# Matmuls on part of TensorE's array are widened to the whole array, with zeros where rows were missing

## The chip, the cores and the metric

The kernel runs on one core of a Trainium2 chip. The metric is the device time of one execution in microseconds (us): 2548.41, the median of three runs (2547.5 to 2549.49).

## The reference

Two transformer-like layers act on 512 tokens of width 1024, all in 32-bit floats. The first has a pooling branch, a gated delta rule with 8 heads of 128 and a product-key expert layer. The second has a state-space scan with 16 heads of 64 and a stick-breaking attention with 16 heads of 64. Three pieces matter here:

```python
# delta rule and scan: decay between two positions of a chunk, per head
diff = gc[..., :, None] - gc[..., None, :]
decay = jnp.where(tril, jnp.exp(jnp.where(tril, diff, 0.0)), 0.0)
# stick breaking, per head
logits = jnp.einsum('bqhd,bkhd->bhqk', q, k) * scale
log_fail = jnp.where(mask, jax.nn.log_sigmoid(-logits), 0.0)
between = lax.cumsum(log_fail, axis=3, reverse=True) - log_fail
w = jnp.where(mask, jnp.exp(jax.nn.log_sigmoid(logits) + between), 0.0)
out = jnp.einsum('bhqk,bkhd->bqhd', w, v)
```

## The kernel before

Activations are kept with features on partitions. A projection takes a slab of weights (128 x 1024), brought by SyncE's DMA into `raw`, rounded by ScalarE into a high part `wh`, whose rest `wl` is made by GpSimd or VectorE; then 24 matmuls of 512 columns add high x high, high x low and low x high into one PSUM tile (`pf` by features, `pt` by tokens). The order of all instructions is fixed when the program is written: generators are advanced between matmuls by a model of time (`K.mm` adds the matmul's columns, `Engine` the VectorE and ScalarE work), and inside each engine the order is then kept. `K.mm` (line 175) counts columns and type alone.

TensorE's array has 128 rows (the contraction, operand partitions) and 128 columns (outputs, PSUM partitions). The profile prints both for each matmul: 64*128 is 64 rows and 128 columns.

The change touches three helpers and their callers.

- `widen`, `decay_rows` and `decay` (lines 1506 to 1530): for H heads the per-token rates are copied to columns 0 to H-1 and 32 to 32+H-1 of a zeroed tile `gw`. `decay_rows` multiplies them with a triangle into `pgr`, rows 0 to 32+H-1, and ScalarE copies these into `gr`, in a rounded high part and, on rows 32 and up, a low part made by VectorE. `decay` then makes one head's table `pd`: a mask by a bf16 matmul, plus a matmul whose stationary operand is one column of `pick`, repeated 128 times, over 40 (H = 8, delta heads) or 48 (H = 16, scan) partitions; `pick` has a one in rows h and 32+h of column h and zeros elsewhere. ScalarE exponentiates `pd` into `DT`. Eight heads do this near 59 to 76 us and 266 to 277 us, sixteen from 1952 to 2019 us, each between projection matmuls.
- `qk_slab` in `block2_` (line 1624): a slab gives queries or keys of two heads, 64 features each. Head 0 has partitions 0 to 63, head 1 has 64 to 127. Tiles `qa` and `qb` hold a head's high part; for queries the other 64 partitions get the low part by a DMA, for keys they get the high part again. The keys' low parts lie in one tile `ql` for both heads.
- `stick` (line 1951): one generator for each of the two heads ("lanes"), over 8 feature slabs; a unit below is one lane in one slab, 16 in all. Its steps: masks (`msb`, 4 bf16 matmuls) and logits, `psb`, for four key blocks of 512, 384, 256 and 128 queries, each with a full matmul (high and repeated keys against high and low queries) and one over the head's 64 partitions (low keys); VectorE and ScalarE make softplus, in high and low parts `sbh`, `sbl`; the cumulative sum on TensorE with a triangle `trilr` and a block of minus ones `nonesr`, into the same `psb`; the exponential `sbw` on ScalarE; the weighted values, four f32 matmuls (two passes each in the trace) with 64 columns of the values `v2t`; and a product with the gate, `og`, on VectorE. Steps of the two lanes stand among the 24 matmuls of the next slabs' projections.

```python
# L1971: logits of one key block, full and half
self.mm(ps[:, c:c + n], k[:, ks], q[:, kb * 128:512], start=False, stop=False, skip_group_check=True)
self.mm(ps[:, c:c + n], kl[ds, ks], q[ds, kb * 128:512], start=False, stop=False, skip_group_check=True)
```

Of the kernel before, what the change touches and what calls it, by code (L numbers as in the profile page):

```python
# [9 lines left out]
F32 = mybir.dt.float32  # L10
F32R = mybir.dt.float32r
# [13 lines left out]
NT = 4  # L25
H1 = 8
# [62 lines left out]
class K:  # L89
# [568 lines left out]
    def decay_rates(self, pba, narrow):  # L658
        yield from narrow
        nc, sm = self.nc, self.sm  # L660
        sh = [128, NT, H1]
        beta = sm.tile(sh, F32, name="beta")
        nc.scalar.activation(beta, pba[:, :, 0:8], AF.Exp, scale=-1.0)
        nc.vector.tensor_scalar(beta, beta, 1.0, None, op0=OP.add)
        nc.vector.reciprocal(beta, beta)
        al = sm.tile(sh, F32, name="al")
        nc.vector.tensor_tensor(al, pba[:, :, 8:16],
                                self.row[:, None, R_DTB:R_DTB + 8].to_broadcast(sh), OP.add)
        g = sm.tile(sh, F32, name="g")
        self.softplus(sm, g, al, "sp1")  # L670
        ea = sm.tile([128, H1], F32, name="ea")
        nc.scalar.activation(ea, self.row[:, R_AL:R_AL + 8], AF.Exp)
        nc.vector.scalar_tensor_tensor(out=g, in0=g, scalar=-1.0, in1=ea[:, None, :].to_broadcast(sh),
                                       op0=OP.mult, op1=OP.mult)
        gw = self.wk.tile([128, 512], F32, name="gw", tag="cy", bufs=5)
        gw = gw[:, :NT * (32 + H1)].rearrange("p (n h) -> p n h", n=NT)
        self.widen(gw, g, H1)
        yield from self.dve(0.3)
        gr = sm.tile([128, 512], F32R, name="gr")
        self.decay_rows(gr, gw, H1, 4)  # L680
        pg = self.pmm.tile([128, 2, NT * H1], F32, name="pg", tag="sc", bufs=4)
        self.mm(pg[:, 0, :], self.triu, g, start=True, stop=True)
        self.mm(pg[:, 1, :], self.ones, g, start=True, stop=True)
        ng = sm.tile(sh, F32, name="ng")
        nc.scalar.activation(ng, pg[:, 0, :], AF.Copy, scale=-1.0)
        eg = sm.tile(sh, F32, name="eg")
        nc.scalar.activation(eg, pg[:, 0, :], AF.Exp)
        egl = sm.tile(sh, F32, name="egl")
        nc.scalar.activation(egl, pg[:, 1, :], AF.Exp)
        gd = sm.tile(sh, F32, name="gd")  # L690
        nc.vector.tensor_tensor(gd, pg[:, 1, :], ng, OP.add)
        edl = sm.tile(sh, F32, name="edl")
        nc.scalar.activation(edl, gd, AF.Exp)
        neg = sm.tile(sh, F32, name="neg")
        nc.vector.tensor_scalar(neg, eg, -1.0, None, op0=OP.mult)
        self.dn.update(beta=beta, gr=gr, ng=ng, eg=eg, neg=neg, egl=egl, edl=edl)
        self.dump("d_beta", beta); self.dump("d_g", g)
# [814 lines left out]

    def decay_rows(self, gr, gw, nh, bufs):

        nc = self.nc
        ps = self.pmm.tile([128, 512], F32, name=self.nm("pgr"), tag="sc", bufs=bufs)
        for n in range(NT):
            self.mm(ps[0:32 + nh, n * 128:n * 128 + 128], gw[:, n, :], self.triu, start=True, stop=True)
        nc.scalar.copy(gr[0:32 + nh], ps[0:32 + nh])
        nc.vector.tensor_tensor(gr[32:32 + nh], ps[32:32 + nh], gr[32:32 + nh].bitcast(F32), OP.subtract)  # L1520

    def decay(self, pd, gr, nh, col, nb, out):

        nc = self.nc
        self.mm(pd, self.identb, self.mnegb[:, None, :].to_broadcast([128, NT, 128]),
                start=True, stop=False, skip_group_check=True)
        self.mm(pd, self.pick[0:32 + nh, col:col + 1].to_broadcast([32 + nh, 128]),
                gr[0:32 + nh].rearrange("p (n i) -> p n i", n=NT), start=False, stop=True, skip_group_check=True)
        for n in range(NT):
            nc.scalar.activation(out[:, n, :], pd[:, n, :], AF.Exp, bias=nb[:, n, col:col + 1])  # L1530

# [4 lines left out]
    def block2_(self):  # L1536
        nc, a, tc, sm, big = self.nc, self.a, self.tc, self.sm, self.big
# [3 lines left out]
        with ExitStack() as ctx:  # L1541
            wk = self.wk = ctx.enter_context(tc.tile_pool(name="swk", bufs=1))
# [13 lines left out]
            zt, yt, vt, og = TK("zt", "A"), TK("yt", "B"), TK("v2t", "H"), B8("og", "D")  # L1556
# [29 lines left out]
            for i in range(4):  # L1586
                self.proj_tok("w_z2_t", i, xn,
                              lambda t, ps, i=i: self.silu2(zt[:, t:t + 2, i * 256:i * 256 + 256], ps),
                              tag=("mm" if i else "sd", 2))
            for i in range(4):  # L1590
                self.proj_tok("w_v2_t", i, xn,
                              lambda t, ps, i=i: nc.scalar.copy(vt[:, t:t + 2, i * 256:i * 256 + 256], ps))
# [16 lines left out]
        with ExitStack() as ctx:  # L1609
            wk = self.wk = ctx.enter_context(tc.tile_pool(name="bwk", bufs=1))  # L1610
# [8 lines left out]
            nc.scalar.preload_act_table_set("natural_log_exp_and_others")  # L1619
            self.qk = {}  # L1620
            lanes = [self.stick(s_, vt, og, oh, ol) for s_ in range(2)]
            go = lambda s_: next(lanes[s_], None)

            def qk_slab(f, which, mid):
                def put(j, ps):

                    scale = (0.125, 1.0)[which]
                    T = lambda n, b=1: wk.tile([128, 512], F32R, name=self.nm(n), tag=f"{n}{which}", bufs=b)
                    hl, lo = (T("qa"), T("qb", 2 - which)), T("ql")
                    half = (slice(0, 64), slice(64, 128))  # L1630
                    for s_ in range(2):
                        nc.scalar.activation(hl[s_][half[s_]], ps[half[s_]], AF.Copy, scale=scale)
                        if which:
                            nc.scalar.dma_start(out=hl[s_][half[1 - s_]].bitcast(F32), in_=hl[s_][half[s_]].bitcast(F32))

                    def rest():
                        for s_ in range(2):
                            nc.vector.scalar_tensor_tensor(out=lo[half[s_]], in0=ps[half[s_]], scalar=scale,
                                                           in1=hl[s_][half[s_]].bitcast(F32), op0=OP.mult, op1=OP.subtract)
                        if not which:  # L1640
                            for s_ in range(2):
                                nc.sync.dma_start(out=hl[s_][half[1 - s_]].bitcast(F32), in_=lo[half[s_]].bitcast(F32))
                    self.rest = rest
                    self.qk[f, which] = hl, lo
                self.proj_feat("w_in2_t", [12 + 2 * f + which], xn, put, mid=mid)
# [53 lines left out]
        with ExitStack() as ctx:  # L1699
            wk = self.wk = ctx.enter_context(tc.tile_pool(name="cwk", bufs=1))  # L1700
            self.pmm = ctx.enter_context(tc.tile_pool(name="cps", bufs=1, space=PSUM))
            out = TK("out2", "F")
# [92 lines left out]
    def scan_rates(self, xn):  # L1795

        nc, a, sm, wk = self.nc, self.a, self.sm, self.wk
# [3 lines left out]
        T = lambda n, dt=F32: sm.tile(sh, dt, name=n)  # L1801
        r = self.sr = {n: T(n) for n in ("dt", "ncs", "ecs", "egl", "dtd")}

        def rates():
# [9 lines left out]
            nc.vector.scalar_tensor_tensor(out=ad, in0=r["dt"], scalar=-1.0, in1=ea[:, None, :].to_broadcast(sh),  # L1814
                                           op0=OP.mult, op1=OP.mult)
            gw = wk.tile([128, 512], F32, name="gw2", tag="cy", bufs=5)
            gw = gw[:, :NT * 48].rearrange("p (n h) -> p n h", n=NT)
            self.widen(gw, ad, 16)
            yield from self.dve(0.8)
            r["gr"] = wk.tile([128, 512], F32R, name="gr2", tag="gr2")  # L1820
# [130 lines left out]
    def stick(self, s_, vt, og, oh, ol):  # L1951

        nc, wk = self.nc, self.wk
        ds = slice(64 * s_, 64 * s_ + 64)
# [3 lines left out]
        W = lambda n, dt=F32: wk.tile([128, 1280], dt, name=self.nm(n), tag=n, bufs=1)  # L1958
        for f in range(8):
            q, (k, kl) = self.qk[f, 0][0][s_], self.qk[f, 1]  # L1960
            k = k[s_]
            ps = self.pmm.tile([128, 3, 512], F32, name=self.nm("psb"), tag=f"sb{s_}", bufs=1)
            ps = ps.rearrange("p b c -> p (b c)")
            for kb in range(NT):
                c, n = seg[kb]
                self.mm(ps[:, c:c + 128], self.identb, self.msb, start=(kb != 3), stop=False, skip_group_check=True)
            for kb in range(NT):
                c, n = seg[kb]
                ks = slice(kb * 128, kb * 128 + 128)
                self.mm(ps[:, c:c + n], k[:, ks], q[:, kb * 128:512], start=False, stop=False, skip_group_check=True)  # L1970
                self.mm(ps[:, c:c + n], kl[ds, ks], q[ds, kb * 128:512], start=False, stop=False, skip_group_check=True)  # L1971
            e = W("sbe")
            for p in parts:
                nc.vector.tensor_scalar(e[:, p], ps[:, p], 60.0, None, op0=OP.min)
# [3 lines left out]
            hi, lo = W("sbh", F32R), W("sbl", F32R)  # L1978
# [7 lines left out]
            for t_ in (hi, lo):  # L1986
                for kb in range(NT):
                    c, n = seg[kb]
                    for kk in range(kb, NT):
                        cc, nn = seg[kk]  # L1990
                        self.mm(ps[:, c + n - nn:c + n], self.trilr if kk == kb else self.nonesr, t_[:, cc:cc + nn],
                                start=False, stop=(kk == NT - 1 and t_ is lo), skip_group_check=True)
            e = W("sbw")
            for p in parts:
                nc.scalar.activation(e[:, p], ps[:, p], AF.Exp)
            yield
            h = 2 * f + s_
            for kb in range(NT):
                c, n = seg[kb]
                self.mm(ps[ds, kb * 128:512], vt[:, kb, h * 64:h * 64 + 64], e[:, c:c + n],  # L2000
                        start=(kb == 0), stop=(kb == NT - 1), skip_group_check=True)
            nc.vector.tensor_tensor(og[ds, f, :], og[ds, f, :], ps[ds, 0:512], OP.mult)
            if s_:
# [119 lines left out]
```

## Time and profile before

| what | value |
|---|---|
| runs, median | 2548.41 us |
| profiled execution, its time | 2550.09 us |
| its span on the core | 2548.3 us |
| TensorE matmuls (PE) busy | 2459.3 us, 97%, 13497 instructions |
| weight loads (PEld) | 2108.3 us, 83% |
| VectorE (DVE) | 1709.0 us, 67% |
| ScalarE (ACT) | 994.0 us, 39% |
| GpSimd (POOL) | 656.2 us, 26% |
| chain of waits that ended last | PE 86%, DVE 11%, issue 2% |

A matmul's row shows its start and a modelled length; matmuls are pipelined, so the distance from one start to the next is the time that one takes, not the length. In square brackets stands how long the engine was idle before an instruction and who released it; "issue" is idle time for which the profile shows no wait.

### The profile page before, as it was taken

Reading aid. Unit: us, or ns where it says so; the run is one execution under the profiler, and the core shown is the slowest. Engines: PE = TensorE matmul, PEld = TensorE weight load, DVE = VectorE, ACT = ScalarE, POOL = GpSimd, SP = SyncE. Lnnn points to the kernel's source line nnn. Section 1 sums busy time; section 2 is a strip of 40 time slices with the busy share of each in tenths; the row PEclk is TensorE's granted clock in tenths of the full one; section 3 lists DMA queues with packets and bytes.
Section 4 is the critical chain, followed back from the end, with each engine's and each line's share of the span. In section 5 each row is a group of like instructions: output and inputs, shape, how many; then the busy total and the mean of one; then the engine's idle time right before and its main releaser. Section 6 shows DMA issues by size and latency. Waiting matters only on the chain.

```text
span 2548.3 us, 34826 instructions
## 1 busy us (share of the span) xinstructions
PE 2459.3 (97%) x13497; PEld 2108.3 (83%) x13497; DVE 1709.0 (67%) x3123; ACT 994.0 (39%) x1453; POOL 656.2 (26%) x401
## 2 busy tenths in 40 slices
PE   6999999989989999999999999999799999999997
PEld 5888788888989999999888888888678988776787
DVE  6776776558998988987577777777754430455433
ACT  4532522332245546455333333333432342444432
POOL 0000000014652222322232323322335234311142
PEclk9999999999999999999999999999899999999999
DMA  3231231324778989889999999998222123222122
GB/s 116 73 93 59 77 110 50 125 101 131 245 269 295 339 286 346 317 315 360 347 326 345 334 343 340 338 323 276 78 67 67 59 91 99 78 60 63 50 91 92
DMA packets 184982, 482.41 MB, mean 189 GB/s; under 512 B 26992, under 2 KB 77296, under 8 KB 184816
## 3 DMA queue, kind: packets, MB, share of 16 engines
q1 hardware_dynamic: 143856, 342.80, 39.5%
q0 software_dynamic: 36864, 134.23, 14.6%
q10 hardware_dynamic: 4096, 3.15, 0.6%
q8 instruction: 106, 1.74, 0.3%
q14 instruction: 60, 0.49, 0.1%
HBM read 422.45 MB, written 53.48 MB: 187 GB/s over the span
## 4 chain that ended last, share of the span: by engine, by line
PE 86%; DVE 11%; issue 2%; ACT 1%; DMA 1%; POOL 0%; SPq 0%; ACTq 0%; DVEq 0%; POOLq 0%
PE pf L175 27%; PE y L175 20%; PE pa L175 18%; PE pt L175 7%; PE psb L175 5%; DVE hn L74 3%; PE pg L175 2%; DVE wl L74 1%; PE tp L180 1%; PE pd L175 1%; PE pyd L175 1%; PE pz L175 1%; DVE oh L74 1%; DVE rt L74 0%; DVE h_out L74 0%
## 5 line engine op out<-in xcount | busy, mean ns | idle before, releaser
L74 ACT CAST wh<-raw 128x1024 fp32r<-128x1024 f32 x310 | 326.4, 1053 | 681.1 <-PE pf L175 303.3
L273 POOL TENSOR_TENSOR wl<-raw,wh 128x1024 fp32r<-128x1024 f32 x113 | 275.9, 2442 | 1047.7 <-ACT wh L74 1029.2
L175 PE MATMUL y<-wh,whl 128*128 128x512 f32 x1524 | 418.0, 395 | 3.9 <-ACT whl L74 3.9
L74 DVE TENSOR_TENSOR wl<-raw,wh 128x1024 fp32r<-128x1024 f32 x197 | 240.9, 1224 | 181.7 <-ACT wh L74 181.6
L175 PE MATMUL pa<-hnh,wl 128*128 128x384 f32 x1024 | 345.2, 337 | 11.0 <-DVE wl L74 5.5
L175 PE MATMUL pa<-hnh,wh 128*128 128x384 f32 x1024 | 347.6, 340 | 3.1 <-ACT st L74 3.1
L175 PEld LDWEIGHTS y<-wh,whl 128*128 128x128 f32 x1524 | 287.4, 189 | 72.3 <-ACT whl L74 4.3
L175 PE MATMUL pa<-hnl,wh 128*128 128x384 f32 x1024 | 343.4, 335 | 0.0
L1480 POOL DMA_INDIRECT ringv<-up,eid x128 | 171.1, 1337 | 422.6 <-DVE h_out L74 388.1
L1480 POOL DMA_INDIRECT ringu<-down,eid x128 | 156.3, 1221 | 355.4 <-DVE hn L74 335.2
L175 PE MATMUL y<-wl,whl 128*128 128x512 f32 x762 | 240.3, 396 | 0.0
L175 PEld LDWEIGHTS pa<-hnh,wl 128*128 128x128 f32 x1024 | 192.7, 188 | 15.7 <-DVE wl L74 7.8
L175 PEld LDWEIGHTS pa<-hnh,wh 128*128 128x128 f32 x1024 | 192.7, 188 | 3.5 <-ACT st L74 3.4
L175 PEld LDWEIGHTS pa<-hnl,wh 128*128 128x128 f32 x1024 | 192.8, 188 | 0.0
L175 PE MATMUL pf<-xnh,wh 128*128 128x512 f32 (+1 forms) x432 | 176.3, 409 | 2.6 <-DVE cy L74 1.7
L74 DVE SCALAR_TENSOR_TENSOR hn<-ringu,hn 128x1024 f32<-128x1024 f32 x128 | 175.0, 1367 | 0.0
L175 PEld LDWEIGHTS y<-wl,whl 128*128 128x128 f32 x762 | 143.6, 189 | 34.7 <-DVE wl L74 0.7
L175 PE MATMUL pf<-x2h,wh 128*128 128x512 f32 (+1 forms) x424 | 169.1, 399 | 2.9 <-DVE cy L74 1.2
L175 PE MATMUL pf<-xnh,wl 128*128 128x512 f32 (+1 forms) x432 | 167.8, 388 | 0.0
L74 DVE SCALAR_TENSOR_TENSOR h_out<-ringv,wgt,h_out 128x1024 f32<-128x1024 f32 x128 | 166.6, 1301 | 0.0
L175 PE MATMUL pf<-xnl,wh 128*128 128x512 f32 (+1 forms) x432 | 166.2, 385 | 0.0
L175 PE MATMUL pf<-x2h,wl 128*128 128x512 f32 (+1 forms) x424 | 166.0, 391 | 0.0
(464 smaller groups left out, 4799.6 us busy)
## 6 DMA issues: line engine op xcount, KB each, us to landing
raw<-w_in_t SPq DMA_DIRECT2D x104, 512.0 KB
raw<-down_t SPq DMA_DIRECT2D x82, 512.0 KB
raw<-up_t SPq DMA_DIRECT2D x55, 512.0 KB
hn<-up_t SPq DMA_DIRECT2D x49, 512.0 KB
Ad<-st SPq DMA_DIRECT2D x32, 768.0 KB
Gd<-stg SPq DMA_DIRECT2D x48, 512.0 KB
ar<-Ad SPq DMA_DIRECT2D x32, 768.0 KB
gr<-Gd SPq DMA_DIRECT2D x32, 768.0 KB
```

Of the source, the lines that this page charges most:

```text
L74: return f(*args, **kw)
L175: self.nc.tensor.matmul(ps, l, r, **kw)
L180: self.nc.tensor.transpose(ps, src, ident)
L273: low = lambda: eng.tensor_tensor(l, raw, h.bitcast(F32), OP.subtract)
L1480: nc.gpsimd.indirect_dma_start(out=(ru, rv)[kind][:, s % 4, :], out_offset=None, in_=a[("down", "up")[kind]], in_offset=bass.IndirectOffse ...
```

## The change

The half-array operands become whole ones. The decay operand `gw` gets 128 columns per chunk instead of 40 or 48, `pgr` and `gr` all 128 rows, and the row-picking matmul contracts over 128 partitions. The keys' low parts get a tile for each head, `klow0` and `klow1`, whose other half is zeroed once; the low logits contract over 128 partitions. The weighted values are made for both heads of a slab (128 columns of `v2t`), and the lane's own half is used.

```diff
@@ decay_rates (and the same edit in scan_rates, gw2)
-        gw = gw[:, :NT * (32 + H1)].rearrange("p (n h) -> p n h", n=NT)
+        gw = gw.rearrange("p (n h) -> p n h", n=NT)
@@ decay_rows
-            self.mm(ps[0:32 + nh, n * 128:n * 128 + 128], gw[:, n, :], self.triu, start=True, stop=True)
-        nc.scalar.copy(gr[0:32 + nh], ps[0:32 + nh])
+            self.mm(ps[:, n * 128:n * 128 + 128], gw[:, n, :], self.triu, start=True, stop=True)
+        nc.scalar.copy(gr, ps)
@@ decay
-        self.mm(pd, self.pick[0:32 + nh, col:col + 1].to_broadcast([32 + nh, 128]),
-                gr[0:32 + nh].rearrange("p (n i) -> p n i", n=NT), start=False, stop=True, skip_group_check=True)
+        self.mm(pd, self.pick[:, col:col + 1].to_broadcast([128, 128]),
+                gr.rearrange("p (n i) -> p n i", n=NT), start=False, stop=True, skip_group_check=True)
@@ block2_, before the slabs
+            klow = [wk.tile([128, 512], F32R, name=f"klow{s_}") for s_ in range(2)]
+            for s_ in range(2):
+                nc.vector.memset(klow[s_][64 - 64 * s_:128 - 64 * s_].bitcast(F32), 0.0)
@@ qk_slab
-                    hl, lo = (T("qa"), T("qb", 2 - which)), T("ql")
+                    hl, lo = (T("qa"), T("qb", 2 - which)), klow if which else [T("ql")] * 2
@@ stick
-            k = k[s_]
+            k, kl = k[s_], kl[s_]
...
-                self.mm(ps[:, c:c + n], kl[ds, ks], q[ds, kb * 128:512], start=False, stop=False, skip_group_check=True)
+                self.mm(ps[:, c:c + n], kl[:, ks], q[:, kb * 128:512], start=False, stop=False, skip_group_check=True)
...
-                self.mm(ps[ds, kb * 128:512], vt[:, kb, h * 64:h * 64 + 64], e[:, c:c + n],
+                self.mm(ps[:, kb * 128:512], vt[:, kb, f * 128:f * 128 + 128], e[:, c:c + n],
```

TensorE's instructions keep their order. Two other engines get another one. On VectorE, at the start of the stick stage, before:

```order
L74 TENSOR_SCALAR nonesr<-ones 128x128
L74 SCALAR_TENSOR_TENSOR ql_17965<-pf_17933,qa_17963 64x512
L74 SCALAR_TENSOR_TENSOR ql_17965<-pf_17933,qb_17964 64x512
L74 SCALAR_TENSOR_TENSOR ql_18004<-pf_17972,qa_18002 64x512
L74 SCALAR_TENSOR_TENSOR ql_18004<-pf_17972,qb_18003 64x512
```

The first pair makes the low parts of slab 0's queries, the second those of its keys. The same place on VectorE, with the change:

```order
L74 TENSOR_SCALAR nonesr<-ones 128x128
L74 MEMSET klow_17933 64x512
L74 MEMSET klow_17934 64x512
L74 SCALAR_TENSOR_TENSOR ql_17969<-pf_17937,qa_17967 64x512
L74 SCALAR_TENSOR_TENSOR ql_17969<-pf_17937,qb_17968 64x512
L74 SCALAR_TENSOR_TENSOR klow_17933<-pf_17976,qa_18006 64x512
L74 SCALAR_TENSOR_TENSOR klow_17934<-pf_17976,qb_18007 64x512
```

Two zeroings stand ahead of the first queries' low parts, and the keys' low parts go to a tile for each head. On ScalarE, in the second layer's scan rates (`cy`, a step of the convolution; `wh`, a weight slab's cast; `gr`, the copy of the decay rows):

```order
 L74 ACTIVATE cy_15463<-pf_15371,vec 128x512
-L74 CAST gr_15493<-pgr_15494 48x512
-L74 ACTIVATE ncs<-pg_15501 128x64
-L74 ACTIVATE ecs<-pg_15501 128x64
-L74 ACTIVATE egl<-pg_15501 128x64
+L74 CAST wh_15493<-raw_66 128x1024
+L74 CAST gr_15499<-pgr_15500 128x512
+L74 ACTIVATE ncs<-pg_15507 128x64
+L74 ACTIVATE ecs<-pg_15507 128x64
+L74 ACTIVATE egl<-pg_15507 128x64
 L74 ACTIVATE dtd<-dtd 128x64
-L74 CAST wh_15510<-raw_66 128x1024
```

The cast of the next weight slab moves from behind the decay rates to ahead of the decay rows' copy, because the longer zeroing moves the model's time there.

## Rows read from the trace of the kernel before

**Rows 1.** Busy time by stretch: start:end, us, engines (x instructions), granted clock, DMA share, GB/s.
```profile
2190.00:2420.00 230.00, 229.10 (x1055) 162.15 (x1054) 128.58 (x182) 108.39 (x155) 42.63 (x18) 0.99 0.20 58
```

**Rows 2.** Waits of TensorE, 2190 to 2420 us: us in total, times, longest.
```profile
PE psb L175 <- DMA qa<-qa: 0.9, 1, 0.9
```

**Rows 3.** Timeline (start, length, instruction, rows*columns, shape), TensorE: logits of one unit.
```profile
2216.02 0.47 PE L175 MATMUL psb<-qa,qa 128*128 128x512 f32 x1
2216.43 0.50 PE L175 MATMUL psb<-qa,ql 64*128 64x512 f32 x1
...
2218.74 0.50 PE L175 MATMUL psb<-sbh,trilr 128*128 128x512 f32 x1
```

**Rows 4.** Timeline of TensorE: the low part's cumulative sum, and the projection after it.
```profile
2220.16 0.44 PE L175 MATMUL psb<-sbl,trilr 128*128 128x512 f32 x1
...
2221.45 0.27 PE L175 MATMUL psb<-sbl,trilr 128*128 128x128 f32 x1
2221.56 0.44 PE L175 MATMUL pf<-x2h,wh 128*128 128x512 f32 x1
```

**Rows 5.** Timeline of TensorE: weighted values of one unit between projection matmuls.
```profile
2224.13 0.39 PE L175 MATMUL pf<-x2h,wl 128*128 128x512 f32 x1
2224.45 2.37 PE L175 MATMUL psb<-sbw,v2t 128*64 128x512 f32 x8
2226.75 0.50 PE L175 MATMUL pf<-x2h,wh 128*128 128x512 f32 x1
2227.09 0.40 PE L175 MATMUL pf<-x2l,wh 128*128 128x512 f32 x1
...
2229.37 0.39 PE L175 MATMUL pf<-x2h,wl 128*128 128x512 f32 x1
```

**Rows 6.** Timeline of TensorE in the scan: full f32 matmuls between projection matmuls.
```profile
1929.44 1.88 PE L175 MATMUL pyo<-St,bc 128*128 128x512 f32 x4
1930.76 0.68 PE L175 MATMUL pt<-wh,x2l 128*128 128x256 f32 x1
1931.28 0.28 PE L175 MATMUL pt<-wl,x2h 128*128 128x256 f32 x1
1931.40 0.28 PE L175 MATMUL pt<-wh,x2h 128*128 128x256 f32 x1
```

**Rows 7.** Timeline of TensorE: decay of a delta head, and of a scan head.
```profile
71.32 0.39 PE L175 MATMUL pd<-mnegb,identb 128*128 128x512 bf16 x1
71.64 0.50 PE L175 MATMUL pd<-gr,pick 40*128 40x512 f32 x1
72.06 0.50 PE L175 MATMUL pf<-xnh,wh 128*128 128x512 f32 x1
72.40 0.39 PE L175 MATMUL pf<-xnl,wh 128*128 128x512 f32 x1
...
1967.61 0.39 PE L175 MATMUL pd<-mnegb,identb 128*128 128x512 bf16 x1
...
1968.35 1.10 PE L175 MATMUL pyd<-xt,DT 128*128 128x64 f32 x8
```

**Rows 8.** Timeline of ScalarE: the exponential that the weighted values at 2224.45 read.
```profile
2222.50 1.30 ACT L74 ACTIVATE sbw<-psb 128x512 f32<-128x512 f32 x2
```

**Rows 9.** Timeline in the second layer's scan rates, VectorE and TensorE.
```profile
1864.94 0.22 DVE L74 MEMSET gw<- 128x192 f32 x1
...
1865.64 1.05 PE L175 MATMUL pgr<-triu,gw 128*48 128x128 f32 x8 [1.98 <-DVE gw L74]
...
1868.47 0.77 PE L175 MATMUL pf<-x2h,wh 128*128 128x512 f32 x1 [1.19 <-DVE cy L74]
...
1869.04 0.63 PE L175 MATMUL pf<-x2l,wh 128*128 128x512 f32 x1
...
1873.73 0.63 PE L175 MATMUL pf<-x2h,wh 128*128 128x512 f32 x1
```

**Rows 10.** Timeline of VectorE at the start of the stick stage.
```profile
2184.86 0.68 DVE L74 SCALAR_TENSOR_TENSOR ql<-pf,qa 64x512 fp32r<-64x512 f32 x1 [4.99 <-ACT qb L74]
```

More of the change, by code (lines that the diff above doesn't have):

```diff
@@ L1637, in rest @@
                         for s_ in range(2):
-                            nc.vector.scalar_tensor_tensor(out=lo[half[s_]], in0=ps[half[s_]], scalar=scale,
+                            nc.vector.scalar_tensor_tensor(out=lo[s_][half[s_]], in0=ps[half[s_]], scalar=scale,
                                                            in1=hl[s_][half[s_]].bitcast(F32), op0=OP.mult, op1=OP.subtract)
@@ L1641, in rest @@
                             for s_ in range(2):
-                                nc.sync.dma_start(out=hl[s_][half[1 - s_]].bitcast(F32), in_=lo[half[s_]].bitcast(F32))
+                                nc.sync.dma_start(out=hl[s_][half[1 - s_]].bitcast(F32), in_=lo[s_][half[s_]].bitcast(F32))
                     self.rest = rest
@@ L1816, in rates @@
             gw = wk.tile([128, 512], F32, name="gw2", tag="cy", bufs=5)
-            gw = gw[:, :NT * 48].rearrange("p (n h) -> p n h", n=NT)
+            gw = gw.rearrange("p (n h) -> p n h", n=NT)
             self.widen(gw, ad, 16)
@@ L1996, in stick @@
             yield
-            h = 2 * f + s_
             for kb in range(NT):
                 c, n = seg[kb]
-                self.mm(ps[ds, kb * 128:512], vt[:, kb, h * 64:h * 64 + 64], e[:, c:c + n],
+                self.mm(ps[:, kb * 128:512], vt[:, kb, f * 128:f * 128 + 128], e[:, c:c + n],
                         start=(kb == 0), stop=(kb == NT - 1), skip_group_check=True)
```

## The prediction

> **What bounds the kernel now.** I read the busy time by stretch first, then the list of waits, then the timeline of TensorE, because the edits touch three places only: the stick-breaking stage (about 2190 to 2420 us), the decay matmuls of the state-space scan, and those of the delta heads near the start. In the stick stage TensorE is busy for 229.10 of 230 us at a clock of 0.99, VectorE for 128.58 and ScalarE for 108.39 [rows 1]; the only wait that TensorE's matmuls have there is one of 0.9 us [rows 2]. So time that TensorE spends there without producing columns is time of the kernel. The order of TensorE's instructions is the same before and after, and so is the set of waits in it; what changes is how many rows or columns of the array an instruction fills.
>
> The timeline shows what that is worth. The logits of one head and one feature slab are eight matmuls, full ones (128*128) and half ones (64*128) in turn, of 512, 512, 384, 384, 256, 256, 128 and 128 columns. They take 2216.02 to 2218.74, 2.72 us for 2560 columns [rows 3]. The cumulative sums right behind are ten full matmuls, also 2560 columns, with two different weight tiles in turn: 2220.16 to 2221.56, 1.40 us [rows 4]. Same engine, same PSUM tile, same kind of operand, same clock; the difference is that no neighbour differs in size. I read the extra 1.3 us as a gap at every change between a half and a full array, about 0.17 us at each of eight changes.
>
> **The sum, part by part.**
> 1. Logits. With full arrays each should run at the pitch of a steady stream: 0.228 us for 512 columns (ten matmuls from 2227.09 to 2229.37 [rows 5]), 0.12 for 256 [rows 6], 0.11 for 128 (2221.45 to 2221.56 [rows 4]), and, an estimate by columns, 0.171 for 384. Twice the four is 1.26 us; the ten cumulative ones, at 1.40, are the other bound. I take 1.30, nearer to the eight-matmul sum because there are fewer weight changes. Saved: 2.72 - 1.30 = 1.42 us for each of 16 units (8 slabs, two heads), 22.7 us. By the bounds, 21.1 to 23.4.
> 2. Weighted values. Eight passes with 64 of 128 output columns. From the last projection matmul before them (2224.13) to the second one after (2227.09) it is 2.96 us [rows 5]. A full-size control of the same type (f32, four passes of 512 columns, then 256-column matmuls) needs 1.84 us from its start to the second matmul after it, which is 4 x 0.43 + 0.12: no gap on leaving [rows 6]. So the new one should be 0.228 + 2560 x 0.43 / 512 + 0.228 = 2.61, and 0.35 us is saved, 16 times: 5.7 us. The low bound counts only what is seen at the two ends, 0.32 and 0.34 instead of 0.228 [rows 5], 0.2 us each time: 3.2. The weights double to 128 columns, but each pass in the control hides such a load.
> 3. Decay, scan: from the mask matmul to the first matmul after the row-picking one 0.74 us (1967.61 to 1968.35), against 2 x 0.228: 0.28 us for each of 16 heads, 4.5 us [rows 7].
> 4. Decay, delta heads: mask, pick and the next projection matmul take 71.32 to 72.40, 1.08 us, against 3 x 0.228: 0.40 us for 8 heads, 3.2 us [rows 7]. These could be lost to a later wait, so the low bound is 0.
> 5. Against it: the zeroing of the decay operand grows from 160 or 192 to 512 columns. It takes 0.22 us at 192, and TensorE waits for it, 1.98 us, before the scan's decay rows [rows 9]; a VectorE operation with 512 columns takes 0.68 [rows 10]. So 0 to 0.5 us more at each of two places; I take 0.3, together -0.6.
> 6. At nothing: the two new zeroings of the low key tiles stand before an operation for which VectorE idles 4.99 us [rows 10]; at 0.68 each they fit. If that cover went, they would cost 1.4 us, once. The wider copy of the decay rows has the same 512 columns per partition. The ScalarE weight cast that moves ahead of the decay rows falls into time in which TensorE and ScalarE both wait for VectorE [rows 9]; it could cost or give a microsecond, and I count 0. No DMA is added or moved.
>
> The sum is 22.7 + 5.7 + 4.5 + 3.2 - 0.6 = 35.5 us. The profiled execution took 2550.09 us around a span of 2548.3, so its like would take 2514.6. It lies 1.68 us over the median of the runs, 2548.41; against that the forecast is **2513 us**. The bounds give savings of 21.1 + 3.2 + 4.5 + 0 - 1.0 = 28 and 23.4 + 5.7 + 4.5 + 3.2 = 37. Uncounted is that the matmul behind the one that follows may come late too: behind the delta heads' picks that one takes 0.34 instead of 0.228 [rows 7], and if it did so behind 16 logits, 16 scan heads and the two decay-row products, 34 x 0.11 = 3.7 us more would be saved. So 28 to 40 us: 2508 to 2521.
>
> **What gets late next.** The stage's 230 us are 14.4 for each of 16 units, and would be 14.4 - 1.42 - 0.35 = 12.6. VectorE's 128.58 us are 8.0 for a unit and ScalarE's 6.8 [rows 1]: no bound. The tightest chain is the last exponential: it ends at 2222.50 + 1.30 = 2223.80 [rows 8], and the weighted values that read it start at 2224.45, a slack of 0.65 us. Both ends hang on the end of the logits, so the faster logits move both; the matmuls between them do not change.
>
> **A rule that speaks against it.** In the trace a half matmul and its neighbour start 0.41 us apart where 512 columns alone take 0.228 [rows 3, 5]: nothing runs beside anything. The Trainium skill, in "TensorE: Matmul & The Clock Gate", Part 3 on packing small matmuls, says that matmuls on different row groups of the array run at the same time, and that a small contraction costs no less than a full one by itself. By that page filling the array would give up overlap and gain nothing; the trace does not agree, since no overlap is there to lose. Without such overlap that page's price for the change is nought, and with it the fourth rival's.
>
> **Rivals.**
> - The gap is not from the size but from changing the weights, or from adding twice into one PSUM place. Then the logits stay at 2.72, and 35.5 - 22.7 = 13 us are saved: 2536. Against it: rows 4 have both and no gap. 5%.
> - Another engine becomes the bound: the exponential of [rows 8] comes later than its slack. Each unit would lose what exceeds 0.65 us; with 0.5 us lost, 16 x 0.5 = 8 us: 2521. 7%.
> - Slower, by the clock: after waits of 1.98 and 1.19 us in the scan's rates, matmuls of 512 columns go at 0.43 us instead of 0.228 for eleven pitches (1869.04 to 1873.73), 2.2 us lost beside the waits of 3.2 [rows 9]. If the faster unit made TensorE wait so at each of 16 units, 16 x 5.4 = 86 us would stand against 35.5: 2599. It would begin to be slower once a unit loses over 2.2 us. For it: the trace shows such a fall. Against it: the slack of 0.65 does not shrink. 2%.
> - Slower, by lost overlap, the rule above: the low half of the logits would be added work, 16 x 0.63 = 10 us: 2558. 1%.
> - It does what it says, but the pitch stays as it is, because the gap belongs to something that I don't see: 2548. 2%.
>
> **How the numbers follow.** My forecast has 83%. The range reaches from 2506 (the best bound, and 2 us for the spread of the runs, 2547.5 to 2549.49) to 2525 (the second rival with 0.75 us lost per unit, 12 us). About 0.2%, 5 us, is what can be told from no change: faster 0.95 (forecast and the first two rivals), the same 0.02, slower 0.03.
>
> **What would show it.** Right: the eight logits of a unit take about 1.3 us, no "issue" idle time stands before their weight loads, a unit recurs 1.8 us sooner than before, and the matmul behind a row-picking one starts 0.23 us after it. Wrong: logits still over 2 us; or TensorE waiting for ScalarE's exponential before the weighted values; or pitches of 0.43 us for 512 columns in the stick stage.

## The result, and the profile after

The changed kernel takes 2515.8 us, the median of four runs (2513.56 to 2519.31). Beside it, on the same chip, the kernel before took 2547.95 (2547.0 to 2549.49). The ratio is 0.9871 (95%: 0.9859 to 0.9883): 32 us less, where 35.5 were forecast. The profiled executions lie 36.5 us apart (spans of 2548.3 and 2511.8 us). A second set of runs, below, gave 35.2.

The page of the changed kernel, the busy times of the engines and the chain that ended last by engine:

```profile
PE 2420.9 (96%) x13497; PEld 2114.1 (84%) x13497; DVE 1714.8 (68%) x3125; ACT 994.0 (40%) x1453; POOL 654.7 (26%) x401
PE 85%; DVE 11%; issue 2%; ACT 1%; DMA 1%; POOL 0%; SPq 0%; DVEq 0%; ACTq 0%; POOLq 0%
```

The number of matmuls is what it was, 13497, and TensorE's busy time is 38.4 us less. The other engines did the same work, but for two new zeroings on VectorE, which is busy 5.8 us longer; most of that are two of its operations that take longer, as told below. Nothing else became the bound: the chain is TensorE's, as before.

**Logits.** TensorE's timeline in the changed kernel, one unit (answers to [rows 3]):

```profile
2205.18 0.47 PE L175 MATMUL psb<-qa,qa 128*128 128x512 f32 x1
2205.49 0.39 PE L175 MATMUL psb<-qa,klow 128*128 128x512 f32 x1
...
2206.48 0.44 PE L175 MATMUL psb<-sbh,trilr 128*128 128x512 f32 x1
...
2217.16 0.47 PE L175 MATMUL psb<-qb,qb 128*128 128x512 f32 x1
```

The eight take 2205.18 to 2206.48, 1.30 us, where they took 2.72; 1.30 was the forecast. The next unit starts 2217.16 - 2205.18 = 11.98 us later. In the kernel before, the logits that follow those at 2216.02 start at

```profile
2229.81 0.47 PE L175 MATMUL psb<-qb,qb 128*128 128x512 f32 x1
```

which is 13.79 us later, so a unit gives 1.81 (1.77 forecast).

**Weighted values.** The same timeline, the values of a unit between projection matmuls (answers to [rows 5]):

```profile
2211.82 0.39 PE L175 MATMUL pf<-x2h,wl 128*128 128x512 f32 x1
2212.05 2.32 PE L175 MATMUL psb<-sbw,v2t 128*128 128x512 f32 x8
2214.12 0.48 PE L175 MATMUL pf<-x2h,wh 128*128 128x512 f32 x1
2214.43 0.39 PE L175 MATMUL pf<-x2l,wh 128*128 128x512 f32 x1
```

From the last projection matmul ahead to the second one behind it is 2.61 us (2211.82 to 2214.43), the forecast to the hundredth; before it was 2.96. The exponential that they read, on ScalarE, is this one (answer to [rows 8]):

```profile
2210.34 1.30 ACT L74 ACTIVATE sbw<-psb 128x512 f32<-128x512 f32 x2
```

It ends at 2211.64, so the slack ahead of the values at 2212.05 is 0.4 us; it was 0.65.

**Decay.** The same timeline, one scan head and one delta head (answers to [rows 7]):

```profile
69.89 0.39 PE L175 MATMUL pd<-mnegb,identb 128*128 128x512 bf16 x1
...
70.57 0.39 PE L175 MATMUL pf<-xnl,wh 128*128 128x512 f32 x1
...
1959.69 0.39 PE L175 MATMUL pd<-mnegb,identb 128*128 128x512 bf16 x1
1959.73 0.58 PE L175 MATMUL pd<-gr,pick 128*128 128x512 f32 x1
1960.15 1.00 PE L175 MATMUL pyd<-xt,DT 128*128 128x64 f32 x8
1960.96 0.36 PE L175 MATMUL pt<-wh,x2l 128*128 128x256 f32 x1
```

Mask and pick of a scan head take 1959.69 to 1960.15, 0.46 us instead of 0.74; for a delta head mask, pick and the next matmul take 0.68 instead of 1.08. The eight matmuls behind a scan head's pick are shorter too: 0.81 us to the next projection matmul (1960.15 to 1960.96). In the kernel before, the pick and that projection matmul started at

```profile
1967.93 0.49 PE L175 MATMUL pd<-gr,pick 48*128 48x512 f32 x1
...
1969.26 0.36 PE L175 MATMUL pt<-wh,x2l 128*128 128x256 f32 x1
```

From 1968.35 [rows 7] to 1969.26 is 0.91. The 0.28 us of mask and pick lie ahead of the pick, which starts 0.04 us behind its mask instead of 0.32; from the pick to the next matmul it is 0.42 us in both kernels. So a scan head gives 0.38 us and not 0.28: the 0.1 us that the prediction named as uncounted.

**Waits.** TensorE's waits that changed, in the changed kernel (us in total, times, longest):

```profile
PE pgr L175 <- DVE gw L74: 4.4, 1, 4.4
PE pd L175 <- DVE gr L74: 2.6, 1, 2.6
PE pf L175 <- DVE cy L74: 2.0, 1, 2.0
PE psb L175 <- ACT sbw L74: 1.7, 1, 1.7
```

and in the kernel before, where the last one is not listed:

```profile
PE pf L175 <- DVE cy L74: 2.9, 2, 1.7
PE pd L175 <- DVE gr L74: 2.3, 1, 2.3
PE pgr L175 <- DVE gw L74: 2.0, 1, 2.0
PE ptb L180 <- DVE xsf L74: 0.8, 1, 0.8
```

The wait ahead of the scan's decay rows (`pgr`) grew by 2.4 us, and one for ScalarE's exponential (`sbw`) is new. The prediction had 0.3 for the first and none for the second. In both places a GpSimd subtraction stands beside a VectorE operation; the experiments show this as the cause of the first wait and as a part only of the second. The timeline of the changed kernel ahead of `pgr`, first GpSimd, then VectorE, then TensorE:

```profile
1862.00 2.34 POOL L273 TENSOR_TENSOR wl<-raw,wh 128x1024 fp32r<-128x1024 f32 x1 [3.04 <-ACT wh L74]
```
```profile
1862.08 2.34 DVE L74 SCALAR_TENSOR_TENSOR ad<-dt,ea 128x64 f32<-128x64 f32 x1
1864.48 0.48 DVE L74 MEMSET gw<- 128x512 f32 x1
```
```profile
1865.44 2.05 PE L175 MATMUL pgr<-triu,gw 128*128 128x128 f32 x8 [4.42 <-DVE gw L74]
```

The multiplication `ad` works on 64 columns; before it took 0.23 us. Here it starts 0.08 us behind GpSimd's `wl` and lasts as long, 2.34 us. The zeroing, which the prediction suspected, grew by 0.26 (0.48 against 0.22 in [rows 9]; 0.3 forecast). The kernel before has one such meeting already, some 5 us earlier in VectorE's work for `ad`, in an operation that takes 0.20 us elsewhere, while GpSimd makes a `wl` from 1859.21 to 1861.60; the changed kernel has that one too:

```profile
1859.26 2.40 DVE L74 TENSOR_SCALAR sp<-sp 128x64 f32<-128x64 f32 x1
```

The first exponential of the stick stage, in the changed kernel (GpSimd, VectorE, ScalarE and TensorE):

```profile
2189.79 2.39 POOL L273 TENSOR_TENSOR wl<-raw,wh 128x1024 fp32r<-128x1024 f32 x1 [6.64 <-ACT wh L74]
2189.97 2.64 DVE L74 CAST sbh<-sbe 128x768 fp32r<-128x768 f32 x1
2191.99 0.44 PE L175 MATMUL psb<-sbh,trilr 128*128 128x512 f32 x1
...
2194.95 1.56 DVE L74 TENSOR_SCALAR sbe<-psb 128x512 f32<-128x512 f32 x2
2195.67 2.91 ACT L74 ACTIVATE sbe<-sbe 128x512 f32<-128x512 f32 x4 [4.74 <-DVE sbe L74]
2198.61 1.30 ACT L74 ACTIVATE sbw<-psb 128x512 f32<-128x512 f32 x2
2199.96 2.42 PE L175 MATMUL psb<-sbw,v2t 128*128 128x512 f32 x8 [1.73 <-ACT sbw L74]
```

The cast `sbh`, 0.56 us elsewhere, takes 2.64. The second head's logits are ready at 2191.99, but VectorE reads them (`sbe<-psb`) only at 2194.95; ScalarE's softplus starts on what that gives, and the exponential for the first head is queued behind the softplus on ScalarE. So TensorE waits 1.73 us for a result that itself needs nothing from the second head.

Where the time was saved, by the start of the same instruction in both profiles:

| place | before | after | ahead by |
|---|---|---|---|
| `pgr`, scan's decay rows | 1865.64 | 1865.44 | 0.20 |
| `ptb` after it, the second | 1880.86 | 1878.74 | 2.12 |
| first logits of the stick stage | 2192.13 | 2183.63 | 8.50 |
| second | 2202.24 | 2190.69 | 11.55 |
| third | 2216.02 | 2205.18 | 10.84 |
| fourth | 2229.81 | 2217.16 | 12.65 |
| end of the span | 2548.3 | 2511.8 | 36.5 |

The steps of 3.05 and -0.71 between the first three logits are the two unexpected things of that stage: the loss above and a gain that the last section shows. How far ahead the stage starts is less certain than these starts suggest: the changed kernel's second profile is 7.2 us ahead at the first logits, and that of the kernel with the weighted values alone, where nothing ahead of the stage is changed, 4.1.

### The profile page after: what moved, and what is told of

Its sections match the earlier page's. It is cut to its first block, busy times and chain, and to the rows that moved or that the text cites. A ratio compares the mean times of both kernels' runs of the same rounds, so it can differ in the third digit from the quotient of the medians.

```text
span 2511.8 us, 34828 instructions
## 1 busy us (share of the span) xinstructions
PE 2420.9 (96%) x13497; PEld 2114.1 (84%) x13497; DVE 1714.8 (68%) x3125; ACT 994.0 (40%) x1453; POOL 654.7 (26%) x401
## 4 chain that ended last, share of the span: by engine, by line
PE 85%; DVE 11%; issue 2%; ACT 1%; DMA 1%; POOL 0%; SPq 0%; DVEq 0%; ACTq 0%; POOLq 0%
PE pf L175 28%; PE y L175 21%; PE pa L175 18%; PE pt L175 7%; PE psb L175 4%; DVE hn L74 3%; PE pg L175 2%; DVE wl L74 1%; PE tp L180 1%; DVE oh L74 1%; PE pz L175 1%; PE pyd L175 1%; DVE h_out L74 1%; DVE rt L74 0%; PE pd L175 0%
```

## The experiments

The theories that the expectations name: G, each change between a half and a full array costs TensorE time; W, the cost is that of changing weights or of adding twice into one place; S, a half-array matmul is slow by itself; C, the long wait ahead of `pgr` comes from the moved ScalarE cast, which starts GpSimd's subtraction beside the small VectorE operation.

**One part at a time.** The kernel before, with only the logits' part of the change:

```diff
+            klow = [wk.tile([128, 512], F32R, name=f"klow{s_}") for s_ in range(2)]
+            for s_ in range(2):
+                nc.vector.memset(klow[s_][64 - 64 * s_:128 - 64 * s_].bitcast(F32), 0.0)
...
-                self.mm(ps[:, c:c + n], kl[ds, ks], q[ds, kb * 128:512], start=False, stop=False, skip_group_check=True)
+                self.mm(ps[:, c:c + n], kl[:, ks], q[:, kb * 128:512], start=False, stop=False, skip_group_check=True)
```

> The kernel before with the low keys' tiles alone made whole (one zero-filled tile for each head, contraction over 128 partitions); decay and weighted values stay on part of the array. Theory G (a gap at each change between a part and the whole of the array): the eight logits matmuls of a unit go from 2.72 us to about 1.3, 16 x 1.4 = 22 to 23 us saved, 2525 to 2526 us. Theory W (the gap belongs to changing weights or to adding into the same PSUM place): logits stay at 2.7 us, time within 2 us of before.

Measured: 2526.1 us, ratio 0.9909 (0.9892 to 0.9925) to 2548.47 beside it, 22.4 less. The weights change as often as before, and each PSUM place is added to as often; only the sizes are equal. W falls. The wait of 1.7 us for `sbw` is there too; that for `pgr` is 2.0 as before.

Only the weighted values:

```diff
-                self.mm(ps[ds, kb * 128:512], vt[:, kb, h * 64:h * 64 + 64], e[:, c:c + n],
+                self.mm(ps[:, kb * 128:512], vt[:, kb, f * 128:f * 128 + 128], e[:, c:c + n],
```

> The kernel before with the weighted values alone made for both heads (128 output columns instead of 64). Theory G: two changes per unit fall away, 0.2 to 0.35 us in each of 16 units, 3 to 6 us saved, 2542 to 2545 us. Theory W: the weights are twice as wide and nothing is won, 2548 us or some us more.

Measured: 2541.99 us, ratio 0.9972 (0.9961 to 0.9983), 6.5 less; the term was 5.7. W falls here too. Whether 64 output columns are slow by themselves or only next to 128 was not tried; 0.35 us for two changes of size is as much for each as with the rows.

Only the decay (operand, rows and pick):

```diff
...
-            self.mm(ps[0:32 + nh, n * 128:n * 128 + 128], gw[:, n, :], self.triu, start=True, stop=True)
-        nc.scalar.copy(gr[0:32 + nh], ps[0:32 + nh])
+            self.mm(ps[:, n * 128:n * 128 + 128], gw[:, n, :], self.triu, start=True, stop=True)
+        nc.scalar.copy(gr, ps)
...
-        self.mm(pd, self.pick[0:32 + nh, col:col + 1].to_broadcast([32 + nh, 128]),
-                gr[0:32 + nh].rearrange("p (n i) -> p n i", n=NT), start=False, stop=True, skip_group_check=True)
+        self.mm(pd, self.pick[:, col:col + 1].to_broadcast([128, 128]),
+                gr.rearrange("p (n i) -> p n i", n=NT), start=False, stop=True, skip_group_check=True)
```

> The kernel before with the decay rows alone made whole. Theory G: 24 heads at 0.28 to 0.40 us, 7.7 us saved on TensorE, less the longer zeroing (0.3 us at each of two places) and less what the changed order costs: the cast that now stands ahead of the decay rows starts GpSimd's subtraction earlier, beside a small VectorE operation that TensorE waits for, about 2 us in the profile of the changed kernel. So 2542 to 2544 us; if that collision is chance and does not recur, 2540 to 2541. Theory W: 2549 us or more.

Measured: 2544.39 us, ratio 0.9982 (0.9973 to 0.9992), 4.1 less by the medians; the terms made 7.1 (4.5 + 3.2 - 0.6), and the interval is 2.0 to 6.9. That is clear of W and 0.4 us outside the 2542 to 2544 of G. The ten runs have a mean granted clock of 0.984 to 0.986, the sixteen of the kernel before beside them 0.986 to 0.989: with this part alone TensorE spends more time at half clock. The heads themselves gave their share: from the matmul at 1952.02 to the one at 2020.03 in the kernel before, which holds all sixteen scan heads, it is 6.3 us less in this profile. Which stretches have the lower clock was not settled; the profile shows one, at the first logits of the stick stage, where the clock is at 0.50 and 0.51 over 3 to 9 us behind them, against 3 to 6 in the kernel before. The wait ahead of `pgr` is 4.4 us here too, with an `ad` of 2.33 us. So that wait belongs to the decay's part. The three parts alone add up to 22.4 + 6.5 + 4.1 = 33.0 us, against 32.2 and 35.2 for the whole change: within the scatter of the runs they do not disturb each other.

**The sizes kept, the order changed.** The kernel before, with its half-array operands, but all four full logits ahead of the four half ones:

```diff
                 self.mm(ps[:, c:c + n], k[:, ks], q[:, kb * 128:512], start=False, stop=False, skip_group_check=True)
+            for kb in range(NT):
+                c, n = seg[kb]
+                ks = slice(kb * 128, kb * 128 + 128)
                 self.mm(ps[:, c:c + n], kl[ds, ks], q[ds, kb * 128:512], start=False, stop=False, skip_group_check=True)
```

> The kernel before, all tiles and sizes as they were, with the logits of a unit in another order: first the four full matmuls, then the four half ones, so that the size changes twice instead of eight times. Theory G: six of eight gaps of 0.17 to 0.18 us fall away in each of 16 units, 16 to 17 us saved, 2531 to 2532 us. Theory S (a half matmul is slow by itself, whatever stands before it, and the one after it too): four or five of eight slow ones stay, at most 8 to 10 us saved, 2538 to 2540 us. Theory W: no change.

Measured: 2530.5 us, ratio 0.9925 (0.9909 to 0.9942), 18.0 less. The logits of a unit in its timeline:

```profile
2212.96 0.83 PE L175 MATMUL psb<-qa,qa 128*128 128x512 f32 x4
2213.72 0.86 PE L175 MATMUL psb<-qa,ql 64*128 64x512 f32 x4
2214.51 0.50 PE L175 MATMUL psb<-sbh,trilr 128*128 128x512 f32 x1
```

Four full ones take 0.76 us and four half ones 0.79, together 1.55 instead of 2.72: a half-array matmul among its like costs no more than a full one. S falls for half the rows, G stands: six changes fewer give 1.17 us, 0.19 each. Of the 22.4 us of the logits' part, 18.0 are had without any zeros, by the order alone; the zeros give the rest.

**The long wait ahead of the decay rows.** The second set ran on another chip, with 2549.21 us for the kernel before. First the changed kernel once more, as it is.

> The changed kernel again, for a second profile and on the chip of the next three. Theory G with the collision: 2514 to 2518 us, TensorE waits over 4 us before the scan's decay rows (a VectorE operation of 64 elements lasting over 2 us beside GpSimd's subtraction) and about 1.7 us for the exponential of the first stick unit. If these two waits were chance of one execution, they are at 2.0 and 0 to 0.5 us in this profile.

Measured: 2514.02 us (2511.83 to 2515.47), ratio 0.986 (0.9843 to 0.9876). The two waits recur, 4.4 and 1.7 us.

Then the kernel before, where only the model of time is told that the zeroing has 512 columns; the instructions are the same, and the ScalarE cast moves as it does in the change:

```diff
+        counted, self.counting = self.counting, False
...
+        self.counting = counted
+        if counted:
+            self.done[0] = max(self.done[0], self.t) + 0.07 + 512 * 0.00106
+            self.ready[gw.name] = 0, self.done[0] + 0.1
```

> The kernel before with nothing widened; only the model of time is told that the decay operand's zeroing has 512 columns, so that ScalarE's weight cast moves ahead of the decay rows as in the changed kernel. Theory C (the moved cast starts GpSimd's subtraction beside a VectorE operation that TensorE waits for): TensorE's wait before the decay rows grows from 2.0 to about 4.1 us in the profile, and about 1 us of it is given back by the transposes behind it; the time stays within 2 us of before. Theory Z (the wait grew because the zeroing is longer): 2.0 us stay.

Measured: 2549.08 us, ratio 1.0002 (0.9992 to 1.0011). Its timeline at that place, GpSimd, VectorE and TensorE:

```profile
1862.46 2.34 POOL L273 TENSOR_TENSOR wl<-raw,wh 128x1024 fp32r<-128x1024 f32 x1 [3.04 <-ACT wh L74]
1862.54 2.33 DVE L74 SCALAR_TENSOR_TENSOR ad<-dt,ea 128x64 f32<-128x64 f32 x1
1864.86 0.22 DVE L55 MEMSET gw<- 128x192 f32 x1
...
1865.56 1.91 PE L175 MATMUL pgr<-triu,gw 128*48 128x128 f32 x8 [4.08 <-DVE gw L74]
```

C is shown: without a wider operand, with the small zeroing of 0.22 us, the moved cast alone makes the wait 4.08 us instead of 1.98. And the time does not change. The opposite, the changed kernel with the model told the old size, so that the cast stays where it was; the edit is the one above with this line in place of its like:

```diff
+            self.done[0] = max(self.done[0], self.t) + 0.07 + NT * (32 + nh) * 0.00106
```

> The changed kernel, with the model of time told the old size of the zeroing, so that ScalarE's casts stay where they were before; all arrays are whole. Theory C: the wait before the decay rows falls from 4.4 to about 2.3 us (the old 2.0 and the longer zeroing), a microsecond or two less than the changed kernel, 2512 to 2516 us. Theory Z: 4.4 us stay.

Measured: 2515.46 us, ratio 0.9864 (0.9848 to 0.9881), not told apart from the changed kernel's 2514.02; the microsecond or two that was expected did not show. The waits around this place (1850 to 1900 us of its span):

```profile
PE pgr L175 <- DVE gw L74: 2.3, 1, 2.3
PE pf L175 <- DVE cy L74: 1.3, 1, 1.3
PE ptb L180 <- DVE xsf L74: 0.8, 1, 0.8
```

The long wait is short again, 2.3 us, and two others are back, 1.3 and 0.8, which the order of the change does not have. What the four orders cost is seen from the start of the wait ahead of `pgr` to the second `ptb`:

| kernel | wait | waits behind it | `pgr` to second `ptb` | sum |
|---|---|---|---|---|
| before | 1.98 | 1.97 | 15.22 | 17.20 |
| before, cast moved | 4.08 | 0.0 | 13.33 | 17.41 |
| changed | 4.42 | 0.0 | 13.30 | 17.72 |
| changed, cast kept | 2.30 | 2.1 | 15.32 | 17.62 |

Moving the cast costs 0.1 to 0.2 us at this place, not 2.1. The reason is the two waits behind, of 2.0 to 2.1 us together, which vanish when the first one grows. The clock is not a second reason. Busy times over the whole sum, for the first two kernels of the table (TensorE's matmuls first, the granted clock third from the end):

```profile
1863.66:1880.86 17.20, 13.25 (x54) 10.38 (x53) 10.85 (x21) 5.67 (x11) 4.79 (x2) 0.80 0.15 50
```
```profile
1861.48:1878.90 17.42, 13.34 (x53) 10.89 (x54) 13.21 (x23) 5.73 (x11) 4.42 (x2) 0.80 0.13 45
```

TensorE is busy for 13.2 to 13.3 us at 0.80 or 0.81 in all four. In the changed kernel's second profile the clock there is 0.90 and the sum 16.31: the clock of a single execution moves this place by more than the order of the casts does.

**The exponential in the first unit.** The kernel just told of, and the low part of that one weight slab made by VectorE, so that GpSimd is quiet there:

```diff
+                if not f:
+                    self.l_dve = lambda i: True
...
+                self.l_dve = lambda i: False
```

> As the one with the kept order, and the low part of the one weight slab that collides in the first stick unit is made by VectorE, behind its own work, not by GpSimd beside it. Theory C: the cast of 0.56 us that took 2.64 is short again, TensorE's wait for the first unit's exponential falls from 1.7 us to under 1, and the time is 1 us below the one with the kept order (2511 to 2515). If the wait has another cause it stays at 1.7.

Measured: 2514.55 us, ratio 0.9864 (0.9847 to 0.988): no difference to its neighbours. The expectation of a wait under 1 us was missed. Its timeline, VectorE, ScalarE and TensorE:

```profile
2193.08 0.56 DVE L74 CAST sbh<-sbe 128x768 fp32r<-128x768 f32 x1
...
2194.55 1.22 DVE L74 TENSOR_TENSOR wl<-raw,wh 128x1024 fp32r<-128x1024 f32 x1
2195.10 0.44 PE L175 MATMUL psb<-sbh,trilr 128*128 128x512 f32 x1
...
2197.12 1.56 DVE L74 TENSOR_SCALAR sbe<-psb 128x512 f32<-128x512 f32 x2
...
2202.13 2.42 PE L175 MATMUL psb<-sbw,v2t 128*128 128x512 f32 x8 [1.32 <-ACT sbw L74]
```

The cast has its 0.56 us again, but the subtraction now stands in VectorE's own queue with 1.22 us, and VectorE still reads the second head's logits 2.0 us after they are ready (2195.10 to 2197.12), where it was 3.0 in the changed kernel. The stretched cast was a part of the delay, 0.4 us of the wait; the rest goes with VectorE's queue, which no run took apart. No version here is measurably faster than the changed kernel.

## Why the prediction was right

- **What bounds the kernel**: right. Time that TensorE spends without producing columns was time of the kernel; 32 to 35 us came off it by the medians, and what was lost elsewhere is small beside them.
- **Term 1, logits**: 1.42 us a unit forecast, 2.72 - 1.30 = 1.42 seen; 22.7 us forecast, 22.4 measured with that part alone. Its reading, a gap of about 0.17 us at each change of size, is shown by the reordered logits, where a change removed gave 0.19. The idle time called issue ahead of weight loads for `psb` in the stage fell from 35.4 us to 8.7, and none is left among the logits of the unit at 2205.18, as the prediction asked.
- **Term 2, values**: 0.35 us a unit in both; 5.7 forecast, 6.5 measured alone.
- **Terms 3 and 4, decay**: each head gave what was forecast, and the uncounted 0.1 us behind a scan head's pick was there. The sign was read wrongly: the matmul behind a pick starts 0.42 us after it, as before, and not 0.23; the time came off between mask and pick, which the prediction had only as part of a sum. From mask to the second step behind, a scan head gives 0.38 us, 6.1 for sixteen instead of 4.5. That this part alone measured 4.1 us, less than its terms, goes with the lower clock of those runs; the whole change shows no such shortfall in its second set (35.2).
- **Term 5, zeroings**: 0.26 us at the scan. At the delta heads the wait for `gr` grew from 2.3 to 2.6 us. Forecast were 0.3 each.
- **Term 6, at nothing**: here one row was missed. "The ScalarE weight cast that moves ... could cost or give a microsecond, and I count 0" held in the sum, but its reason did not. The cast did not merely fall into idle time: it started GpSimd's subtraction, which stretched a VectorE operation from 0.23 to 2.34 us, and TensorE's wait grew by 2.1. That this was nearly free comes from the waits behind it. [Rows 9] shows one of them, 1.19 us, but the prediction did not draw on it.
- **The slack of the exponential**: 0.65 us forecast to stay, because "the matmuls between them do not change". It fell to 0.4 us: from the end of the logits to the values it is 5.57 us instead of 5.71, and to the end of the exponential 5.16 instead of 5.06. With logits alone it is 0.49, with values alone 0.56. In the steady units no wait appears, so the second rival gave nothing there; in the first unit it did, 1.7 us once. That wait is one of the prediction's own signs of being wrong; it came once, where the rival needed it in each unit.
- The other rivals fall: W by the logits alone, lost overlap because the kernel became faster (and each full matmul takes all 128 rows, so that full and half ones have no separate rows here), the fall of the clock because no wait recurs by unit, and "the pitch stays" by the 1.30 us.

The terms ahead of the stick stage, 6.1 + 3.2 for the heads less 0.3 and the 0.5 us of the table above (17.72 - 17.20), make 8.5; the first logits start 8.50 us sooner. That the two agree so closely is luck, since the changed kernel's second profile has 7.2 there. The stage gives the rest: 28.0 us seen, 28.4 forecast, and the second profile has 28.0 too. Here a gain of 1.5 us by the clock and a loss of 2.5 in the second unit (14.49 us instead of 11.98), neither of them forecast, cancel in part. Against the median of the first runs the forecast of 2513 is 2.8 us low, and against the second set's 1.0; the four runs of the first set alone differ by 5.8, with a mean granted clock from 0.984 (2519.31 us) to 0.987 (2513.56), so that remainder is not assigned to a step.

## What to carry to other kernels

Look in TensorE's timeline for matmuls that alternate between part of the array and all of it: each change of size cost 0.17 to 0.19 us here, as much as 400 columns. Fill the missing rows with zeros where they can be zeroed once, or put equal sizes next to each other, which needs no zeros and gave four fifths of what the logits had to give; a matmul over half the rows among its like was not slow. And when an edit moves one instruction, follow what it starts on the other engines, down to whom that meets there and which waits behind it vanish, before a longer wait is counted as lost.

## What the runs showed that was not expected

A VectorE operation of 64 columns can last as long as the GpSimd subtraction beside it: 2.34 us instead of 0.23 for a multiplication with two SBUF inputs, 2.64 instead of 0.56 for a cast. The Trainium skill, in "SBUF — State Buffer", section "Who interferes with whom", says that VectorE and GpSimd share one pair of ports under an exclusive lock, that a VectorE operation with two SBUF inputs contends with a GpSimd one that reads SBUF, and that casts can take that pair too; these rows agree, and give the size.

TensorE's clock fell in the kernel before where nothing waited. These are busy times by stretch, from 3 to 6 us behind the first logits of the stick stage; the granted clock is the number behind the engines. First the kernel before, then the changed one:

```profile
2195.13:2198.13 3.00, 3.00 (x8) 2.31 (x7) 2.47 (x4) 2.41 (x4) 0.00 (x0) 0.50 0.00 0
```
```profile
2186.63:2189.63 3.00, 3.00 (x15) 2.48 (x14) 2.44 (x5) 2.97 (x4) 0.00 (x0) 1.00 0.02 5
```

0.50 is 1.2 GHz, 1.00 is 2.4. Behind a wait of 0.9 us for a DMA and the 2.7 us of alternating logits, the clock was at half in three of the four profiles that keep those logits (before, decay alone, cast moved; not with values alone). With logits of 1.3 or 1.55 us it was at full in all six. In the kernel before, eight projection matmuls there take 3.36 us (2195.21 to 2198.57) instead of 8 x 0.228 = 1.82: these 1.5 us and the 1.4 of the unit make 2.9 of the step of 3.05 in the table of starts. With one of the four at full clock and nothing else held fixed, ten profiles do not show that the alternating logits are the cause; it was not tried by itself. The two unexpected steps go together: TensorE waits for the first exponential, 0.6 to 1.8 us, in all seven profiles where the clock stayed up, the one with values alone among them, and in none of the three where it fell.
